# Two FFNs whose up projections keep tokens stationary, in a two-block fp32 kernel on one core

## The chip, the cores and the metric

One core of one Trainium2 chip runs the whole kernel. The metric is device time of one execution in microseconds; the time of a kernel is the median of its runs. The engines are TensorE (PE in the views, its weight loads apart as PEld), VectorE (DVE), ScalarE (ACT), GpSimd (POOL) and SyncE (SP), which issues the DMAs here.

## The reference, cut to what matters

256 tokens of width 1024 go through two blocks. The first has a SwiGLU FFN, a mixer (attention and gated linear attention side by side), a second SwiGLU FFN and a gated embedding; the second block has two more mixers and two FFNs with short convolutions. The change touches the two SwiGLU FFNs and the gated linear attention of the first block:

```python
def swiglu(x, w_gate, w_up, w_down):
    return (jax.nn.silu(x @ w_gate) * (x @ w_up)) @ w_down

h = h + 0.5 * swiglu(rmsnorm(h, ffn1_norm), ffn1_w_gate, ffn1_w_up, ffn1_w_down)   # 1024 -> 2816 -> 1024
...                                                                                  # mixer
h = h + 0.5 * swiglu(rmsnorm(h, ffn2_norm), ffn2_w_gate, ffn2_w_up, ffn2_w_down)

def step(state, inp):            # gated linear attention, one chunk
    qi, ki, vi, gi = inp
    b = jnp.cumsum(gi, axis=2)
    diff = b[:, :, :, None, :] - b[:, :, None, :, :]
    decay = jnp.exp(jnp.where(causal, diff, -jnp.inf))
    attn = jnp.einsum('bhid,bhjd,bhijd->bhij', qi, ki, decay)
    ...
```

## The kernel before, in words

All of it is fp32 in and out. A product of fp32 matrices is made of three matmuls in a reduced format: each operand is split into a high part (`hi` of weights, `xh` of activations) and the rest (`lo`, `xl`), and high x high, high x low and low x high are added in PSUM. Weights arrive in halves of 128 x 1024 values (512 KB): `halves` (L584) issues the DMA into `raw` (3 buffers), ScalarE writes `hi` (L470, AF.Copy), VectorE writes `lo` in two pieces (L436); `hi` and `lo` have six buffers each. The very first half is loaded in four pieces of 128 KB (`PIECES`).

There are two forms of projection. `row_units` (L713) keeps **weights** stationary: a half is 8 k slices of 128 hidden columns, and all 256 tokens of `xh` and `xl` move, so a matmul is 128x256; the result has hidden columns on partitions and tokens along the free axis. `col_units` (L694) keeps **tokens** stationary: a half is two k slices of 512 columns, which move, so a matmul is 128x512, once for each of two token halves; the result has 128 tokens on partitions.

`ffn` (L733) works through 11 groups of 256 hidden columns (`NG`), each with 256 columns of gate and of up weights, and then that group's rows of the down weights:

```python
for g in range(NG + 1):
    if g < na:
        self.run_units(self.col_units(src, up_at[g], 512, xh, xl, tok_fin(g)))
    elif g < NG:
        for c in range(2):
            for run in self.row_units(src, up_at[g] + c, xh, xl, row_fin(2 * g + c)):
                run()
    if g > 0:
        self.run_units(down(g - 1), lead=2 if g == NG else 0)
```

`na` is `NA[0]` for the first FFN and `NA[1]` for the second. After a row unit, `row_fin` (L755) scales the PSUM bank by the tokens' norm factors (VectorE, 128x512; the factors were spread over partitions once by two small matmuls), takes silu of the gate half (ScalarE), multiplies gate and up (POOL, since `TTX` is POOL), and splits the product into `hh` and `hl` (ScalarE and VectorE, tiles `halfr`). After a column unit, `tok_fin` (L738), for each token half, takes silu of the gate columns with the norm factor as ScalarE's scale, multiplies with the up columns on VectorE (tile `half`), transposes the product by two 128x128 matmuls against the identity (L524), and splits the transposed product from PSUM. `down` (L776) uses `hh` and `hl` as stationary operands and moves 512 down-weight columns; it is the same in both cases. The host lays the weights out to suit (`_ffn_w`, L1787), so the bytes loaded are the same.

In the first mixer (`mixer1`, L871) the queries of four heads lie in `gq`, a tile of 128 partitions and two halves of 512, the even heads in partitions 0 to 63 of the first half, the odd ones in partitions 64 to 127 of the second; the rest of the tile is zero. `decay_levels` (L812) multiplies queries and keys by decays at seven levels; for the queries this is one VectorE operation for each of the two halves, on 64 partitions.

The order of all instructions is set by a planner (`Plan`, L53 to L372) when the program is built: it gets every operation with its engine, a cost and its dependencies, lists them in an order for each engine by priority, and chooses the buffer of each tile. Each engine then takes its own instructions strictly in that order. So a change of form anywhere can move instructions elsewhere.

Of the kernel before, what the change touches and what calls it, by code (L numbers as in the profile page):

```python
# [14 lines left out]
P = 128  # L15
# [6 lines left out]
NEG = -1.0e30  # L22
LEVELS = [1, 2, 4, 8, 16, 32, 64]
LEAD = 2
RING = 6
RAW = 3
BANKS = {"a": 8}
BANK = {"m": "a", "t": "a"}
BKEEP = 0
NA = (0, 1)  # L30
RKEEP = 1
HKEEP = 3
OKEEP = 999
# [340 lines left out]
class Kern:  # L374
# [209 lines left out]
    def halves(self, src, idx, width, gain_k=None):  # L584

        def prep(h):
            hw = width // 2
            raw = self.plan.tile("raw", [P, 1024], F32, RAW, RKEEP)
            np_, self.pieces = self.pieces, 1
            for j in range(np_):  # L590
                z = slice(j * hw // np_, (j + 1) * hw // np_)
                self.dma(raw[:, z], src[idx][:, h * hw:(h + 1) * hw][:, z])
            hi = self.plan.tile("hi", [P, 1024], F32R, RING, RKEEP)
            lo = self.plan.tile("lo", [P, 1024], F32R, RING, RKEEP)
            nq = len(LOPAT) // 2
            q = hw // nq
            m = hw // np_
            for j in range(np_):
                self.act(hi[:, j * m:(j + 1) * m], raw[:, j * m:(j + 1) * m], AF.Copy)
            for j in range(nq):  # L600
                s = slice(j * q, (j + 1) * q)
                r = raw[:, j * q:(j + 1) * q]
                self.tt(lo[:, s], r, hi[:, s].bitcast(F32), ALU.subtract, {"P": "POOL", "V": "DVE", "X": "DVE|POOL"}[LOPAT[h * nq + j]])
            return hi, lo

        return [lambda: prep(0), lambda: prep(1)]

    def run_units(self, units, lead=None):
        lead = LEAD if lead is None else lead

        n, w = len(units), {}
        for i in range(n + lead):
            if i < n:
                w[i] = units[i][0]()
                units[i][1](0, *w[i])
            if i >= lead:
                self.plan.bias = BIAS[self.phase]
                units[i - lead][1](1, *w.pop(i - lead))
                self.plan.bias = 0
# [251 lines left out]
    def mixer1(self, xh, xl, rs):  # L871
# [3 lines left out]
        gk, gf = self.big("gk"), self.big("gf")  # L875
        gk3 = gk.rearrange("p (c t) -> p c t", c=2)

        gq = self.plan.tile("g", [P, D], F32, 2)
        self.mset(gq, 0.0)
        gq4 = gq.rearrange("p (n c t) -> p n c t", n=2, c=2)  # L880
        half = [slice(0, 64), slice(64, P)]
# [148 lines left out]
        def og_fin(t, ps):  # L1030
# [9 lines left out]
        self.run_units(self.col_units(a["w_in1"], 0, 512, xh, xl, qk_fin)  # L1040
                       + self.col_units(a["w_in1b"], 0, 272, xh, xl, kv_fin))
        smat = [self.big("smat").rearrange("p (a t i) -> p a t i", a=2, t=2) for _ in range(2)]
        self.decay_levels([(pp, gq[pp, 512 * n:512 * n + 512]) for n, pp in enumerate(half)], gk3, gf,
                          [[(gk3[:, c], gq4[:, :, c], 0)] for c in range(2)], smat)
        self.run_units(self.col_units(a["w_in1"], 2, 512, xh, xl, attn)
                       + self.col_units(a["w_in1"], 4, 512, xh, xl, v_fin)
# [13 lines left out]
        for t in range(2):  # L1060
            po = [self.psum("a") for _ in range(2)]
            os = [po[h % 2][:, 128 * (h // 2):128 * (h // 2) + 128] for h in range(4)]
            for h in (0, 2, 1, 3):
                c, pp = h // 2, slice(64 * (h % 2), 64 * (h % 2) + 64)
# [626 lines left out]
    def run(self):  # L1691
# [21 lines left out]
        def fin1(t, acc):  # L1713
            self.add_half(t, acc)
            self.to_xt(t, self.hsrc(t), *nx, gi=1)
            nr[t] = self.hnorm(t)
        self.ffn(a["w_ffn1"], NA[0], xh, xl, rs, fin1)
        self.phase = 1
# [5 lines left out]
        def fin2(t, acc):  # L1724
            self.add_half(t, acc)
            self.to_xt(t, self.hsrc(t), *px, gi=3)
            pr[t] = self.hnorm(t)
        self.ffn(a["w_ffn2"], NA[1], *nx, nr, fin2)
        self.phase = 3
# [36 lines left out]
def _c(a):  # L1766
    return np.ascontiguousarray(a)
# [7 lines left out]
def _rows2(w):  # L1775

    n = w.shape[0] // 256
    return w.reshape(n, 2, P, D).transpose(0, 2, 1, 3).reshape(n, P, 2 * D)
# [8 lines left out]
def _ffn_w(wg, wu, wd, na):  # L1787
    up, dn = ffn_order()
    out = np.empty((3 * NG, P, 2048), wg.dtype)
    rows = _rows2(wd)  # L1790
    for g in range(NG):
        s = slice(256 * g, 256 * g + 256)
        if g < na:
            out[up[g]:up[g] + 2] = _cols(np.concatenate([wg[:, s], wu[:, s]], 1), 512)
        else:
            z = [slice(256 * g + P * c, 256 * g + P * c + P) for c in range(2)]
            out[up[g]:up[g] + 2] = _stat(np.concatenate([w[:, c] for c in z for w in (wg, wu)], 1))
        out[dn[g]] = rows[g]
    return out
# [10 lines left out]
def layout(i):  # L1810
# [7 lines left out]
        i["ffn1_norm"][0], i["mix_norm"][0], i["ffn2_norm"][0], i["ple_gate_norm"][0])], 1))  # L1818
    o["w_ffn1"] = _ffn_w(i["ffn1_w_gate"][0], i["ffn1_w_up"][0], i["ffn1_w_down"][0], NA[0])
    win = i["w_in"][0]  # L1820
# [13 lines left out]
    o["w_out1"] = _c(_rows2(np.concatenate([wo[:512].reshape(8, 64, D)[order].reshape(512, D), wo[512:]])))  # L1834
    o["w_ffn2"] = _ffn_w(i["ffn2_w_gate"][0], i["ffn2_w_up"][0], i["ffn2_w_down"][0], NA[1])
    wp = i["ple_w_gate"][0]
# [92 lines left out]
```

## Time and profile before

| | |
|---|---|
| median of 3 runs | 1249.11 us (1245.09 to 1250.49) |
| the profiled execution | 1248.71 us |
| its span, first to last instruction | 1246.9 us |
| PE matmul busy | 1218.3 us (98%) |
| DVE, ACT, POOL busy | 857.1 (69%), 672.4 (54%), 194.5 (16%) us |
| read from HBM | 207.18 MB, 167 GB/s over the span |
| ACT table loads | 17 |

By the tiles that PE works on, the first FFN runs from about 7 to 205 us, the first mixer to about 327, the second FFN to about 520. Busy is an engine's time with an instruction in flight. PE's matmuls overlap (one is shown as lasting longer than the distance to the next start), so its pace is read from starts.

### The profile page before, as it was taken

How to read it: one execution, taken by the hardware profiler on the slowest of the kernel's cores; microseconds unless marked ns; L12 is line 12 of the kernel's file. 1: busy time of each engine (PE TensorE's matmuls, PEld its weight loads, DVE VectorE, ACT ScalarE, POOL GpSimd, SP SyncE). 2: the span in 40 equal slices, each digit the busy share in tenths (PEclk: the TensorE clock that was granted, in tenths of full speed). 3: DMA queues.
4: the chain of work that ended last, by engine and by line, in shares of the span. 5: the costliest groups of instructions: out<-in, count | busy, mean ns of one | idle time of the engine just before them, and what ended most of it. 6: DMA issues, size and time to landing. Idle time of an engine off the chain costs nothing.

```text
span 1246.9 us, 21305 instructions
## 1 busy us (share of the span) xinstructions
PE 1218.3 (98%) x8084; PEld 1101.0 (88%) x8084; DVE 857.1 (69%) x1627; ACT 672.4 (54%) x1125; POOL 194.5 (16%) x247
## 2 busy tenths in 40 slices
PE   7999999999999999999999999999999999999997
PEld 7899998787899999789998799999799887999996
DVE  5665567876755655778687786776868557766776
ACT  5444445764654444557465675555652356655554
POOL 2111010420011111002001011111113521111111
PEclk9999999999999999999999999999999999999999
DMA  8755554425455555552424555555553244555552
GB/s 282 231 185 176 189 180 148 143 94 194 161 181 188 187 183 192 180 165 78 146 75 150 195 174 185 181 196 181 187 190 103 80 158 155 185 179 193 187 194 93
DMA packets 61158, 209.61 MB, mean 168 GB/s; under 512 B 7424, under 2 KB 9728, under 8 KB 60928
## 3 DMA queue, kind: packets, MB, share of 16 engines
q1 hardware_dynamic: 61056, 208.26, 50.6%
q8 instruction: 63, 1.03, 0.3%
q14 instruction: 39, 0.32, 0.1%
HBM read 207.18 MB, written 1.05 MB: 167 GB/s over the span
## 4 chain that ended last, share of the span: by engine, by line
PE 79%; DVE 7%; DMA 5%; ACT 4%; issue 2%; POOL 1%; SPq 0%; DVEq 0%; POOLq 0%; ACTq 0%
PE psa L513 77%; DVE lo L436 3%; ACT hi L470 2%; DMA raw<-in_w_ffn 2%; PE psa L524 2%; DVE big L451 1%; DMA raw<-in_cf_u 1%; DVE big L436 1%; POOL sml L436 1%; ACT big L470 1%; DMA raw<-in_w_out 1%; DMA big<-in_xT 1%; ACT L366 1%; DVE xl L436 0%; DVE c_h L451 0%
## 5 line engine op out<-in xcount | busy, mean ns | idle before, releaser
L436 DVE TENSOR_TENSOR lo<-raw,hi 128x512 fp32r<-128x512 f32 x756 | 506.9, 715 | 244.0 <-ACT hi L470 240.7
L470 ACT ACTIVATE hi<-raw 128x1024 fp32r<-128x1024 f32 x381 | 394.0, 1047 | 336.1 <-PE psa L513 237.1
L513 PE MATMUL psa<-xh,hi 128*128 128x256 f32 x1568 | 448.6, 286 | 7.3 <-ACT hi L470 7.0
L513 PE MATMUL psa<-xh,lo 128*128 128x256 f32 x1568 | 445.3, 284 | 1.3 <-DVE lo L436 1.0
L513 PE MATMUL psa<-xl,hi 128*128 128x256 f32 x1568 | 443.7, 283 | 0.1
L513 PEld LDWEIGHTS psa<-xh,hi 128*128 128x128 f32 x1568 | 298.8, 191 | 16.8 <-ACT hi L470 7.4
L513 PEld LDWEIGHTS psa<-xl,hi 128*128 128x128 f32 x1568 | 298.6, 190 | 9.5 <-DVE xl L436 0.4
L513 PEld LDWEIGHTS psa<-xh,lo 128*128 128x128 f32 x1568 | 298.4, 190 | 3.2 <-DVE lo L436 3.1
L513 PE MATMUL psa<-hi,halfr 128*128 128x512 f32 x720 | 212.0, 395 | 0.5 <-DVE halfr L436 0.4
L436 POOL TENSOR_TENSOR big<-big 128x256 f32<-128x256 f32 (+1 forms) x88 | 90.6, 1031 | 597.3 <-ACT big L470 513.0
L513 PE MATMUL psa<-hi,xh 128*128 128x512 f32 (+1 forms) x368 | 144.4, 411 | 2.2 <-ACT xh L470 1.6
L513 PE MATMUL psa<-lo,xh 128*128 128x512 f32 (+1 forms) x368 | 137.5, 392 | 0.9 <-DVE lo L436 0.8
L513 PE MATMUL psa<-hi,xl 128*128 128x512 f32 (+1 forms) x368 | 135.9, 410 | 2.3 <-DVE xl L436 2.2
L513 PEld LDWEIGHTS psa<-hi,halfr 128*128 128x128 f32 x720 | 121.9, 188 | 15.5 <-DVE halfr L436 1.0
L513 PE MATMUL psa<-lo,halfr 128*128 128x512 f32 x360 | 113.6, 391 | 0.5 <-DVE lo L436 0.5
L513 PE MATMUL psa<-big,big 128*128 128x128 f32 (+8 forms) x652 | 92.9, 274 | 1.3 <-DVE big L436 0.9
L513 PEld LDWEIGHTS psa<-big,big 128*128 128x128 f32 (+6 forms) x652 | 86.8, 188 | 8.2 <-POOL big L436 1.5
L513 PEld LDWEIGHTS psa<-hi,xh 128*128 128x128 f32 x368 | 69.2, 190 | 17.0 <-ACT xh L470 4.9
L513 PEld LDWEIGHTS psa<-lo,xh 128*128 128x128 f32 x368 | 69.7, 189 | 15.0 <-DVE lo L436 3.1
L513 PEld LDWEIGHTS psa<-hi,xl 128*128 128x128 f32 x368 | 68.4, 190 | 16.1 <-DVE xl L436 5.1
L513 PEld LDWEIGHTS psa<-lo,halfr 128*128 128x128 f32 x360 | 67.6, 188 | 16.3 <-DVE lo L436 0.9
L470 ACT ACTIVATE big<-big 128x256 f32<-128x256 f32 (+2 forms) x104 | 45.4, 439 | 59.0 <-DVE big L436 35.2
(167 smaller groups left out, 950.2 us busy)
## 6 DMA issues: line engine op xcount, KB each, us to landing
raw<-in_w_ffn SPq DMA_DIRECT2D x131, 512.0 KB, 4.5
raw<-in_cf_u SPq DMA_DIRECT2D x88, 512.0 KB, 4.2
raw<-in_cf_d SPq DMA_DIRECT2D x44, 512.0 KB, 4.3
raw<-in_w_in SPq DMA_DIRECT2D x16, 512.0 KB, 4.6
raw<-in_w_abB SPq DMA_DIRECT2D x16, 512.0 KB, 3.8
raw<-in_w_cA SPq DMA_DIRECT2D x16, 512.0 KB, 3.9
raw<-in_w_cB SPq DMA_DIRECT2D x16, 512.0 KB, 3.8
raw<-in_w_abA SPq DMA_DIRECT2D x12, 512.0 KB, 4.1
```

What stands on the lines that cost most here:

```text
L366: self.nc.scalar.preload_act_table_set(i)
L436: return eng, c, lambda: self.ew(eng).tensor_tensor(out=out, in0=a, in1=b, op=op), op != ALU.pow and not self.ps_(a, b)
L451: lambda: self.nc.vector.scalar_tensor_tensor(out=out, in0=a, scalar=s, in1=b, op0=op0, op1=op1, accum_out=accum),
L470: self.plan.add([("ACT", c, lambda: self.nc.scalar.activation(out, a, f, scale=scale, **kw))], outs, ins, SETS.get(f))
L513: return [self.nc.tensor.matmul(o, l, r, start=st, stop=sp) for o, l, r, st, sp in lst]
L524: self.plan.add([("PE", 4 + P / 1.2, lambda: self.nc.tensor.transpose(out, a, idn))], [out], [a, idn], cols=P * 2)
```

## The change

`NA` goes from (0, 1) to (11, 11): every group of both FFNs goes through `col_units` and `tok_fin`; before, that was so for the first group of the second FFN alone. The norm factors are no longer spread over partitions for the FFNs. The queries' decay takes all 128 partitions of each half of `gq`, zeros among them. The conversion of a weight half into `hi` gets a lower bound on its number of pieces, which is 1.

```diff
+GW = 1
+HIP = 1
-NA = (0, 1)
+NA = (11, 11)
...
             m = hw // np_
-            for j in range(np_):
+            m = min(m, hw // HIP)
+            for j in range(hw // m):
                 self.act(hi[:, j * m:(j + 1) * m], raw[:, j * m:(j + 1) * m], AF.Copy)
...
-        self.decay_levels([(pp, gq[pp, 512 * n:512 * n + 512]) for n, pp in enumerate(half)], gk3, gf,
+        self.decay_levels([(slice(0, P), gq[:, 512 * n:512 * n + 512]) for n in range(2)] if GW else
+                          [(pp, gq[pp, 512 * n:512 * n + 512]) for n, pp in enumerate(half)], gk3, gf,
```

By count, 2016 matmuls of 128x256 leave PE, 1008 of 128x512 and 84 transposes of the product come, and four small matmuls on the norm factors leave. The order changes throughout the first block and in places of the second; the last 1168 PE instructions of the program stand as before. Three places follow. Names are those of tiles with a number of their buffer; L494 before is L496 after, and so on.

SP at the program's start, before (`big_89` to `big_92` take the input, transposed, two k slices each, `big_89` in two loads of one slice; `raw` takes weight halves, `raw_102` the one in four pieces; `c_h` the residual, 1 MB):

```order
L494 DMA big_89<-in_xT 128x256
L494 DMA raw_114<-in_w_ffn 128x1024
L494 DMA raw_102<-in_w_ffn 128x256 x2
L494 DMA big_90<-in_xT 128x512
L494 DMA big_89<-in_xT 128x256
L494 DMA raw_106<-in_w_ffn 128x1024
L494 DMA big_91<-in_xT 128x512
L494 DMA raw_102<-in_w_ffn 128x256 x2
L494 DMA big_92<-in_xT 128x512
L494 DMA c_h_86<-in_x 128x2048
```

The same place after:

```order
L496 DMA big_89<-in_xT 128x256
L496 DMA raw_106<-in_w_ffn 128x1024
L496 DMA raw_102<-in_w_ffn 128x256 x4
L496 DMA raw_109<-in_w_ffn 128x1024
L496 DMA big_89<-in_xT 128x256
L496 DMA big_90<-in_xT 128x512
L496 DMA c_h_86<-in_x 128x2048
L496 DMA raw_102<-in_w_ffn 128x1024
L496 DMA raw_106<-in_w_ffn 128x1024
L496 DMA raw_109<-in_w_ffn 128x1024
L496 DMA big_91<-in_xT 128x512
L496 DMA big_92<-in_xT 128x512
```

The later k slices of the input moved behind the residual and three more weight halves.

PE in the middle of the first FFN, before (`psa` are PSUM banks; `hi` and `lo` here are stationary where `xh` moves, and `halfr` is stationary where they move):

```order
L513 MATMUL psa_117<-hi_103,halfr_129 128x512
L513 MATMUL psa_125<-hi_103,halfr_129 128x512
L513 MATMUL psa_117<-lo_104,halfr_129 128x512
L513 MATMUL psa_125<-lo_104,halfr_129 128x512
L513 MATMUL psa_137<-xh_87,hi_123 128x256
L513 MATMUL psa_137<-xl_88,hi_123 128x256
L513 MATMUL psa_137<-xh_87,lo_119 128x256
```

PE in a middle group after, from the last up matmuls of one token half (on `psa_105`) to its transposes (of `half_131`):

```order
L515 MATMUL psa_105<-lo_128,xh_87 128x512
L515 MATMUL psa_105<-hi_107,xl_88 128x512
L515 MATMUL psa_129<-hi_113,xh_87 128x512
L515 MATMUL psa_129<-lo_111,xh_87 128x512
L515 MATMUL psa_129<-hi_113,xl_88 128x512
L515 MATMUL psa_132<-hi_125,halfr_140 128x512
L515 MATMUL psa_112<-hi_125,halfr_140 128x512
L515 MATMUL psa_132<-lo_108,halfr_140 128x512
L515 MATMUL psa_112<-lo_108,halfr_140 128x512
L526 MATMUL psa_122<-c_ident_62,half_131 128x128 x2
L515 MATMUL psa_129<-hi_113,xh_87 128x512
```

Seven matmuls of 128x512 stand between the last on `psa_105` and the transposes; before, PE had no transposes in such a group.

ACT in middle groups of the first FFN, before (`big<-big` is the silu):

```order
L470 ACTIVATE hi_126<-raw_114 128x1024
L470 ACTIVATE halfr_121<-big_143 128x256
L470 ACTIVATE big_144<-big_144 128x256
L470 ACTIVATE hi_123<-raw_102 128x1024
L470 ACTIVATE big_145<-big_145 128x256
L470 ACTIVATE hi_107<-raw_106 128x1024
```

And after (`half<-psa,sml` is the silu, one for each token half):

```order
L472 ACTIVATE halfr_133<-psa_122 128x256
L472 ACTIVATE half_137<-psa_105,sml_95 128x256
L472 ACTIVATE halfr_140<-psa_122 128x256
L472 ACTIVATE hi_107<-raw_109 128x1024
L472 ACTIVATE hi_110<-raw_102 128x1024
L472 ACTIVATE hi_113<-raw_106 128x1024
L472 ACTIVATE half_115<-psa_129,sml_99 128x256
```

The weight conversions now come in threes between the endings of the two token halves.

## Rows read from the trace of the kernel before

**Rows 1.** The page: busy us of PE by part 1, the chain by part 4.
```profile
PE 1218.3 (98%) x8084; PEld 1101.0 (88%) x8084; DVE 857.1 (69%) x1627; ACT 672.4 (54%) x1125; POOL 194.5 (16%) x247
...
PE 79%; DVE 7%; DMA 5%; ACT 4%; issue 2%; POOL 1%; SPq 0%; DVEq 0%; POOLq 0%; ACTq 0%
```
**Rows 2.** Stretches: length; PE, PEld, DVE, ACT, POOL busy (count); clock; DMA share, GB/s.
```profile
60.00:187.00 127.00, 127.00 (x897) 119.21 (x896) 75.68 (x120) 57.20 (x75) 12.67 (x15) 1.00 0.57 183
...
297.40:311.00 13.60, 13.60 (x59) 11.07 (x60) 8.11 (x16) 5.61 (x8) 0.00 (x0) 1.00 0.58 189
187.00:345.00 158.00, 154.51 (x856) 128.35 (x855) 116.25 (x235) 96.67 (x190) 29.75 (x44) 1.00 0.45 150
500.00:545.00 45.00, 43.19 (x200) 33.82 (x199) 36.64 (x66) 26.91 (x44) 3.68 (x4) 1.00 0.53 170
```
**Rows 3.** Timeline of PE, second FFN: start us, us, engine, line, operation, tiles, shape.
```profile
328.04 0.40 PE L513 MATMUL psa<-hi,xh 128*128 128x512 f32 x1
...
330.33 0.39 PE L513 MATMUL psa<-lo,xh 128*128 128x512 f32 x1
...
335.07 0.28 PE L513 MATMUL psa<-xh,lo 128*128 128x256 f32 x1
...
339.39 0.28 PE L513 MATMUL psa<-xh,lo 128*128 128x256 f32 x1
```
**Rows 4.** Timeline of PE around four transposes at the first mixer's end.
```profile
324.31 0.40 PE L513 MATMUL psa<-lo,xh 128*128 128x512 f32 x1
324.54 0.60 PE L524 MATMUL psa<-c_ident,c_h 128*128 128x128 f32 x4
...
325.21 0.49 PE L524 MATMUL psa<-c_ident,c_h 128*128 128x128 f32 x3
```
**Rows 5.** Second FFN's first group: tile `half` (ns min/median/max), then ACT's and DVE's timeline.
```profile
L470 ACT ACTIVATE half<-psa,sml x2: 458/466/473, 335.2 to 345.8; 128x256 f32<-128x256 f32 x2
L451 DVE SCALAR_TENSOR_TENSOR half<-psa,sml,half x2: 479/481/483, 335.9 to 346.3; 128x256 f32<-128x256 f32 x2
...
351.47 0.38 ACT L470 ACTIVATE halfr<-psa 128x256 fp32r<-128x256 f32 x1 [1.05 <-PE psa L524]
...
351.89 0.42 DVE L436 TENSOR_TENSOR halfr<-psa,halfr 128x256 fp32r<-128x256 f32 x1
```
**Rows 6.** Groups by line, 60 to 187 us: busy us, mean ns | idle before, releaser.
```profile
L470 ACT ACTIVATE big<-big 128x256 f32<-128x256 f32 x15 | 6.1, 409 | 13.1 <-DVE big L436 13.1
...
L436 DVE TENSOR_TENSOR big<-psa,half 128x512 f32<-128x512 f32 x15 | 10.3, 688 | 6.8 <-PE psa L513 6.6
...
L436 POOL TENSOR_TENSOR big<-big 128x256 f32<-128x256 f32 x15 | 12.9, 861 | 115.3 <-ACT big L470 115.3
```
**Rows 7.** Timeline of the start; the last bracket is idle time before and its releaser.
```profile
5.69 1.67 ACT L470 ACTIVATE hi<-raw 128x1024 fp32r<-128x1024 f32 x3 [1.46 <-DMA raw<-in_w_ffn]
...
6.80 0.58 PE L513 MATMUL psa<-xh,hi 128*128 128x256 f32 x1 [6.80 <-ACT hi L470]
...
9.12 0.58 PE L513 MATMUL psa<-xh,hi 128*128 128x256 f32 x1 [0.37 <-DVE xh L445]
...
9.99 1.06 ACT L470 ACTIVATE hi<-raw 128x1024 fp32r<-128x1024 f32 x1 [1.13 <-DMA raw<-in_w_ffn]
...
14.21 0.41 PE L513 MATMUL psa<-xh,hi 128*128 128x256 f32 x1
...
14.42 0.34 PE L513 MATMUL psa<-xl,hi 128*128 128x256 f32 x1
...
14.60 0.28 PE L513 MATMUL psa<-xh,lo 128*128 128x256 f32 x1
...
15.36 0.63 ACT L470 ACTIVATE junkACT<-c_h 128x512 bf16<-128x512 f32 x1 [2.02 <-DMA c_h<-in_x]
...
19.23 0.28 PE L513 MATMUL psa<-xh,lo 128*128 128x256 f32 x1
```
**Rows 8.** The queries' tile `g` on DVE: ns min/median/max, first and last start.
```profile
L436 DVE TENSOR_TENSOR g<-g,half x12: 275/418/775, 253.7 to 271.3; 64x256 f32<-64x256 f32 x10, 64x128 f32<-64x128 f32 x2
```

## The prediction

> **What bounds the kernel now.** I read the page's busy table and its chain first: TensorE's matmul row is busy 98% of the span, and 79% of the chain that ended last is PE, the rest crumbs of other engines [rows 1]. A busy PE row can hide waiting, so the next view is busy time by stretch [rows 2]. In the middle of the first big FFN (60 to 187 us) PE is never idle, while VectorE is busy 75.68 of 127 us (60%) and ScalarE 57.20 (45%). In the stretch from the end of that FFN through the attention/GLA mixer (187 to 345) PE is idle 158.00 - 154.51 = 3.5 us, and where the second FFN hands over to the gate projection (500 to 545) 1.8 us. The granted clock is 1.00 in all four, the higher of TensorE's two levels (2.4 GHz). So the time is PE's instruction stream, and an edit is worth what it adds to or takes from that stream, plus the few microseconds of waits at its edges. What counts there is not a matmul's duration (they overlap) but the distance from one start to the next, which the timeline gives [rows 3].
>
> **The change part by part.**
>
> *Up projections on PE.* 21 of the 22 hidden groups of the two FFNs change form (the second FFN's first group had the new form already). A group was 2 chunks x 2 halves x 8 k x 3 terms = 96 matmuls of 128x256; it becomes 2 token halves x 8 k x 3 = 48 of 128x512. Starts of 128x256: from 335.07 to 339.39 there are 36 of them, 0.120 us each [rows 3]; from 14.60 to 19.23 there are 39, 0.1187 [rows 7]; I take 0.1195. Starts of 128x512 with tokens stationary: 328.04 to 330.33 holds ten, 0.229 [rows 3]; 59 in 13.60 us are 0.2305 [rows 2]; I take 0.231, which leans to the larger sample. Old: 96 x 0.1195 = 11.47 us. New: 48 x 0.231 = 11.09. Gain 0.38 us a group: halving the count while doubling the width is nearly neutral, because a 256-wide one already costs about half.
>
> *Transposes on PE.* The gated product now has tokens on partitions, so each token half needs two 128x128 transposes, 4 a group. Price: from 324.31 to 325.21 stand two 512-wide matmuls and four transposes [rows 4]: 0.90 - 2 x 0.231 = 0.44, or 0.11 each, although each is shown lasting 0.27. Four cost 0.44 us a group. The net is -0.38 + 0.44 = +0.06 a group, +1.3 us for 21. Four small matmuls that spread the token scale over partitions go away in exchange (two per FFN, at the transposes' 0.11): -0.4. **PE work: +0.8 us.** Ends: 0.229 against 0.120 gives -0.09 a group, -2.3 in all; 0.233 (as far above my value as 0.229 is below it) against 0.1187, with 0.12 per transpose, gives +0.27, +5.2 in all.
> The Trainium skill (TensorE: Matmul & The Clock Gate, "Back-to-back issue gap") gives a gap of N/2.4 + 2.5 ns, so 216 ns for 512 columns and 109 for 256; by it, an estimate, the up matmuls would gain only 0.13 a group and the sum would be 5 us higher. The trace has 231 and 120, and its ratio is what I use.
>
> *The other engines.* Per chunk the old ending cost DVE 0.69, ACT 0.41 and POOL 0.86 us [rows 6] ahead of the split into high and low part. The new one costs, per token half, ACT 0.47 and DVE 0.48 [rows 5]; the split stays, one of each per chunk or half (0.38 and 0.42 [rows 5]). Per group of two chunks or two halves DVE falls by 0.4 us, ACT rises by 0.1, POOL loses 1.7. All three lie beside 17 us of PE work per group (11.47 + 24 down matmuls x 0.231) and none is what PE waits for, so I count nothing. Without that cover the 21 groups would give back up to 8 us on DVE.
>
> *The new wait.* A transpose can't start before silu and product are done, and PE takes its instructions in order, so a late product holds up every matmul behind the transpose. After the last up matmul's slot: its data are done 0.16 us later (0.39 long, 0.23 apart), hand-over 0.04 (ScalarE ends at 351.47 + 0.38, VectorE starts at 351.89 [rows 5]), silu 0.47 and hand-over, product 0.48 and hand-over, 0.11 for the transpose's weight load (no more than their spacing): 1.34 us. In the new order on PE (the second of the three places) seven 512-wide matmuls stand between, 1.62 us, for one token half of every steady group of the first FFN; ten in the second; the other half has over 8 us. So the tight case has 0.28 us in hand. From the transpose to the first down matmul that needs it there are six microseconds or more in steady groups. Price 0.
>
> *The start.* The sequence of loads changes (the first of the three places). Before, PE began at 6.80 us, restarted at 9.12 after waiting for the second k slice of x, ran at half pace (starts 0.21 apart at 14.21, against 0.12 later), and only from 14.60 on at full pace [rows 7]: its 29 matmuls by then are 29 x 0.1195 = 3.5 us of work, so it was 11.1 us behind a PE that never waited. After, the first matmul needs the second load's first two pieces: ScalarE converts one full half and two pieces ahead of it, which took from 5.69 to 7.36 before as well: 7.4. The second slice of x is now behind 1,680 KB instead of 1,168. Taking landings by KB ahead as before (1,808 KB in at 9.99, 3,600 at 15.36 [rows 7], so 334 KB per us): it lands at about 10.0, PE resumes at 10.5 instead of 9.12 (conversion and hand-over between), and the slices four and five, behind 4,880 KB, come at about 19.2. PE: 5 matmuls (0.43 each at half pace) to 9.6, wait to 10.5, 12 more at half pace until about 15.8 (the old one needed 5.3 to 5.5 us from its restart to full pace), 7 at full pace to 17.4, 12 of the second group to 20.2, and the slices of x are then there. 36 x 0.231 = 8.3 done at 20.2: 11.9 behind. **+0.8 us**; ends 0 (full pace at 14.6 as before) and +3.4 (the late slices of x 2.6 us later).
>
> *Queries' decay on 128 partitions.* Sixteen VectorE operations (two over 512 elements, twelve over 256, two over 128) work on all partitions, half of them zeros, instead of 64. A 64x256 one takes 0.418 at the median [rows 8], a 128x256 one 0.42 [rows 5]: the price goes by elements per partition, so 0 (at most 0.1 us in all). The slow ones (up to 0.775) are the second of a pair, behind POOL's decay of the keys, and stay. The constant for conversion pieces changes nothing: the minimum is the old value.
>
> *Edges.* The planner sets a new order around both FFN ends. It can at most remove the 3.5 + 1.8 = 5.3 us of PE idle there, or add as much; I take 0.
>
> **Sum against the profiled execution** (1248.71, of which 1246.9 is span): 1248.71 + 0.8 + 0.8 = 1250.3. That execution was 0.4 below the median of the runs, so the forecast is **1250.7**.
>
> **The rivals.**
> 1. *The transposes wait in place* (slower). The silu is one ScalarE instruction in a queue of weight conversions of about 1.06 us. If it becomes ready just after one has begun, the product is up to 1.06 late, 0.28 of which is covered: 0.78 x 21 halves = 16 us, 1267. It decides from 0.28 us of lateness. Against: in the order the silu of the tight half has a short copy ahead of it, three conversions stand before that, and the one group that already has this form shows no PE wait. The old row form had no such point inside a group.
> 2. *A transpose occupies PE for the 0.27 us that its row shows*: 84 x 0.27 = 22.7, less 8.0 for the up matmuls and 0.4, is +14.3, with the start 1264. This is what the Trainium skill (same page, "Part 4: PE-mode transpose") would say, about 275 ns in a kernel's context and no full clock. Against: the starts of rows 4, 0.11 apart with the next matmul not pushed back.
> 3. *Faster*: the new order hands each token half on as soon as it is done, so that the first half's tail, norm and transposes run under the second half's matmuls, and the idle time at both FFN ends goes (-5.3); with the low end of the PE work (-2.3) and the start as before: 1241.5. For it: all of that idle lies at those hand-overs. Against: the order there still has one half's finish just ahead of the mixer's first projections, as before.
>
> **How the numbers follow.** A measurement of this kernel can tell about 0.5% (6.2 us) from no change. Forecast 0.68 (1246 to 1255, all within 0.5%); rival 1 0.14, rival 2 0.04, rival 3 0.14. Faster 0.14, same 0.68, slower 0.18. The range: down to 1243.5, which leaves out the lower part of rival 3 (0.08), and up to 1260, the sum of the upper ends of PE work and start (1248.7 + 5.2 + 3.4 = 1257.3, with under 3 for the edges), which leaves out rival 2 and the full price of rival 1 (0.12).
>
> **What would show it.** Up matmuls of 128x512 starting 0.23 apart and transposes costing 0.11 between them; PE not idle from 60 to 187; no wait of PE on VectorE's product in the waits view; about 20 us until full pace without a gap over 1 us; decay operations of 128x256 at 0.42. Wrong would be: a wait of the same length repeating once every 17 us (rival 1), a group period above 17.3 us without waits (rival 2), or the stretches 187 to 345 and 500 to 545 shortening by several microseconds (rival 3).

## The result, and the profile after

The changed kernel takes 1259.98 us (median of six runs, 1254.16 to 1265.34), the kernel before in the same series 1249.24 (1245.09 to 1250.49): ratio 1.0098, 95% interval 1.0081 to 1.0114. It is slower by about 1%, twice the 0.5% that the prediction took as what a measurement can tell. A later series gave 1258.61 against 1247.77, ratio 1.0086 (1.0073 to 1.0099). The profiled execution is the shortest of its six, 1254.16 (span 1252.3), 5.4 above that of before; a second profile, of the later series, took 1257.38. The loss differs from execution to execution, so I read both profiles.

The page of the changed kernel, parts 1 and 4, answering to [rows 1], and then the stretches of [rows 2]:

```profile
PE 1221.4 (98%) x7152; PEld 1052.4 (84%) x7152; DVE 839.5 (67%) x1627; ACT 670.5 (54%) x1123; POOL 155.1 (12%) x205
...
PE 70%; DMA 11%; DVE 9%; ACT 5%; issue 3%; POOL 1%; SPq 0%; DVEq 0%; POOLq 0%; ACTq 0%
```
```profile
60.00:187.00 127.00, 126.22 (x558) 101.08 (x557) 64.59 (x115) 55.08 (x73) 0.00 (x0) 1.00 0.56 185
187.00:345.00 158.00, 154.71 (x807) 125.64 (x805) 113.09 (x230) 94.49 (x180) 27.90 (x39) 1.00 0.45 147
345.00:500.00 155.00, 153.98 (x683) 122.53 (x682) 83.59 (x153) 73.90 (x106) 3.91 (x7) 1.00 0.56 181
500.00:545.00 45.00, 43.89 (x206) 34.72 (x204) 36.17 (x68) 28.05 (x48) 3.02 (x4) 1.00 0.56 177
```

PE's busy share is the same 98%, the bytes and the clock are the same (in each of the three profiles the granted clock falls to 0.50, the lower level, once and at the same place, near 892, 895 and 897 us, behind an idle PE of 1.7 to 2.0 us), and DVE and POOL have less to do, as forecast. What changed is the chain: PE's share falls from 79% to 70%, and DMA's rises from 5% to 11% (to 16% in the second profile). PE was never idle in the middle of the first FFN; now it is idle 0.78 us there and 1.02 us in the second.

The chain of one 20-us stretch in the middle of the first FFN (start, us, what) shows where it goes. Before, it is one piece, all PE:

```profile
69.93 20.16 PE psa L513 x140
```

In the changed kernel it leads from load to load:

```profile
69.34 6.03 DMA raw<-in_w_ffn
...
75.45 1.06 ACT hi L472
76.51 0.18 ACT halfr L472
76.69 6.44 DMA raw<-in_w_ffn
...
83.22 1.07 ACT hi L472
...
84.31 0.70 DVE lo L438
...
85.05 5.11 PE psa L515 x21
```

A weight half is loaded (6.4 us), split into `hi` (1.07) and `lo` (0.70), and PE has to wait for it; the load itself could only be issued when an earlier conversion had emptied a `raw` buffer. That is what SyncE's queue waits for in this stretch (60 to 187 us; who waits for whom: us, times, longest):

```profile
SPq L496 <- DVE lo L438: 108.9, 44, 7.4
```

Before, it waited as long for the same thing (110.5 us, 45 times); what differs is when the weights are wanted.

Loads of FFN weights, 60 to 187 us (count, KB each, median us from issue to landing), before and after:

```profile
raw<-in_w_ffn SPq DMA_DIRECT2D x45, 512.0 KB, 4.3
```
```profile
raw<-in_w_ffn SPq DMA_DIRECT2D x43, 512.0 KB, 5.3
```

About as many bytes in the same time, but later landings: in the changed kernel the issues come in threes, 1.2 us apart, and then none for 5 us or more (66.94, 68.14, 69.34, then 75.27, 76.69, 77.91 us, then 85.67). The median distance of two issues between 30 and 190 us is 1.24 us; before it was 2.53. The order says why. Counted in PE's work (0.231 and 0.1195 us a matmul), PE wants a new half after 1.4, 1.4, 6.1, 1.8, 1.4 and 4.8 us in a group of the new form, and after 2.1, 5.4, 1.4, 2.8, 2.3 and 2.9 in the old: a half of up weights now lasts six matmuls of one token half, 1.39 us, where it lasted 24 of 128x256, 2.87 us.

By place, from PE's first transposes of the residual after each stage: the first FFN is 1.0 us longer (2.1 in the second profile), the mixer 0.5 shorter (0.6), the second FFN 3.2 longer (3.3), all that follows 1.8 longer (3.9), though no operation changed there.

In the second FFN (327 to 511 us) neither PE nor its weight loads waited for `hi` or `lo` before; now they do:

```profile
PEld psa L515 <- DVE lo L438: 3.9, 9, 0.5
...
PEld psa L515 <- ACT hi L472: 0.8, 3, 0.4
```
```profile
PE psa L515 <- DVE lo L438: 0.8, 4, 0.2
```

In the first FFN, from 30 to 190 us, the waits of PE and of its weight loads for `hi` and `lo` add up to 4.7 us (4.0 in the second profile), but to 3.7 before as well: there the old form is hardly better supplied.

### The profile page after: what moved, and what is told of

Read it like the earlier page. It is cut to its first block, busy times and chain, and to the rows that moved or that the text cites. A ratio compares the mean times of both kernels' runs of the same rounds, so it can differ in the third digit from the quotient of the medians.

```text
span 1252.3 us, 19425 instructions
## 1 busy us (share of the span) xinstructions
PE 1221.4 (98%) x7152; PEld 1052.4 (84%) x7152; DVE 839.5 (67%) x1627; ACT 670.5 (54%) x1123; POOL 155.1 (12%) x205
## 4 chain that ended last, share of the span: by engine, by line
PE 70%; DMA 11%; DVE 9%; ACT 5%; issue 3%; POOL 1%; SPq 0%; DVEq 0%; POOLq 0%; ACTq 0%
PE psa L515 67%; DMA raw<-in_w_ffn 7%; DVE lo L438 4%; ACT hi L472 4%; PE psa L526 3%; DMA raw<-in_cf_u 2%; DVE big L453 1%; POOL sml L438 1%; DMA raw<-in_w_in 1%; DMA raw<-in_w_out 1%; DVE big L438 1%; DMA c_h<-in_x 1%; DVE c_h L453 1%; DVE xl L438 0%; DVE big L486 0%
## 5 line engine op out<-in xcount | busy, mean ns | idle before, releaser
L515 PE MATMUL psa<-hi,xh 128*128 128x512 f32 (+1 forms) x704 | 280.7, 408 | 10.7 <-ACT hi L472 8.0
L515 PE MATMUL psa<-lo,xh 128*128 128x512 f32 (+1 forms) x704 | 272.3, 396 | 1.7 <-DVE lo L438 1.5
L515 PE MATMUL psa<-hi,xl 128*128 128x512 f32 (+1 forms) x704 | 263.2, 406 | 1.7 <-DVE xl L438 1.6
L515 PE MATMUL psa<-xh,hi 128*128 128x256 f32 x896 | 257.1, 287 | 0.1
L515 PE MATMUL psa<-xh,lo 128*128 128x256 f32 x896 | 253.4, 283 | 1.1 <-DVE lo L438 1.1
L515 PE MATMUL psa<-xl,hi 128*128 128x256 f32 x896 | 252.5, 282 | 0.3 <-DVE xl L438 0.3
L515 PEld LDWEIGHTS psa<-xl,hi 128*128 128x128 f32 x896 | 170.1, 190 | 5.4 <-DVE xl L438 0.8
L515 PEld LDWEIGHTS psa<-xh,hi 128*128 128x128 f32 x896 | 169.9, 190 | 4.9 <-ACT hi L472 0.3
L515 PEld LDWEIGHTS psa<-xh,lo 128*128 128x128 f32 x896 | 169.8, 189 | 2.1 <-DVE lo L438 1.9
L515 PEld LDWEIGHTS psa<-hi,xh 128*128 128x128 f32 x704 | 133.1, 190 | 40.4 <-ACT hi L472 10.0
L515 PE MATMUL psa<-lo,halfr 128*128 128x512 f32 x360 | 113.3, 391 | 0.0
```

The source lines that it names most:

```text
L515: return [self.nc.tensor.matmul(o, l, r, start=st, stop=sp) for o, l, r, st, sp in lst]
```

## The experiments

My theory A: the column form wants weights in bursts, so PE waits for halves that land late, differently in each execution. Against it stood B (the order that the planner chose elsewhere, above all in the second block), C (the decay) and D (PE's own work, mis-priced).

**The changed kernel again, and its parts one by one.**

```diff
-NA = (11, 11)
+NA = (0, 1)
```
for the decay alone; for one FFN alone `NA = (11, 1)` or `NA = (0, 11)` with `GW = 0`.

> The changed kernel once more, for its spread and a second profile. Theory A (weight supply): in the column form the first token half takes four new weight halves, 2 MB, in 24 matmuls (24 x 0.231 = 5.5 us), and all four stay in their buffers until the second token half has used them; so PE has little weight in hand and waits whenever a load lands late, a different amount in each execution. Then this profile shows more waits of PE on the weights' hi and lo inside the two FFNs than the first one did (seven of 0.3 to 0.7 us there), the more the longer this execution is; median 1260, spread 8 to 11 us. Theory B (the order around the mixers and in the second block): the additional time lies outside the two FFNs. Theory D (PE's own work mis-priced): the time inside the FFNs is the same in every execution, and so is the total to about 3 us.

> The kernel before with the queries' decay on 128 partitions alone, both FFNs as before. Theories A and D (the FFNs' form): 1249, ratio 1.000 within 0.002. Theory C (the decay, with the order that it makes the planner choose): some or all of the 11 us, 1252 to 1260.

> Only the first FFN in the column form, 11 groups; the second FFN and the decay as before. Theory A: 11 of 21 groups, so about half of the loss, 1254 to 1255, and a wider spread than the kernel before (5 us). Theory D: the same half, but with the spread of the kernel before. Theory B: anything, the loss not in proportion to the groups, and outside 14 to 200 us.

> Only the second FFN in the column form (ten groups more than before); the first FFN and the decay as before. Theory A: about half of the loss, 1254 to 1255, with waits on hi and lo between 345 and 500 us. Theory D: the same half, without such waits. Theory B: the loss not in proportion; with the first-FFN kernel the two do not add up to 11 us.

Measured: 1258.61 again (1257.38 to 1259.73, so the spread was narrow this time, and A's sign is missing: the second profile is 3.2 us longer than the first, but its waits on `hi` and `lo` are not more, 4.0 against 4.7 us in the first FFN and 3.7 against 5.5 in the second); decay alone 1250.86, ratio 1.0027 (1.0012 to 1.0041); first FFN alone 1258.33, 1.0081 (1.0068 to 1.0094); second alone 1253.00, 1.0044 (1.0031 to 1.0056); before 1247.77. The parts, 3.1 + 10.6 + 5.2 us, add up to far more than the whole, 10.8. So A is not all: B has a share. In the profile of the kernel with the first FFN alone, that FFN is 2.1 us longer than before, but the mixer 2.4 and what follows the second FFN 5.7. The decay, which I had priced at nothing, costs 3 us although its operations do not (their median is 0.422 us at 128x256, 0.418 before at 64x256 [rows 8]); in its profile the first block is 1 us shorter than before and what follows 2 us longer.

**Old and new orders put together.** To hold the order of a block fixed, the planner got a list for each engine, made from a plan of the other kernel, and might place an operation of those phases only if it was next on its list.

```diff
+    for x in model.order():
+        if not isinstance(x, str) and x[0] in to:
+            guide[model.ops[x[0]][0][x[1]][0]].append(to[x[0]])
+    trial.guide = guide
     order = trial.order()
...
                 for i in c:
+                    if i in held and self.guide[e][nextg[e]:nextg[e] + 1] != [i]:
+                        continue
```

> The changed kernel, its first block planned as in it, but in the second block (from the second mixer on) every engine takes its instructions in the order of the kernel before. Theory B (a part of the loss is the new order in the second block, where no operation changed): in two profiles of the changed kernel that block is 1.7 and 3.8 us longer than before, so this kernel is 2 to 4 us faster than the changed one, 1254 to 1256. Theory A alone (weight supply in the FFNs): no gain, 1258.

> The other way round: both FFNs, the decay and the first block's order as before, the second block in the order of the changed kernel. Theory B: the second block's share alone, 1250 to 1252. Theory A alone: 1248, the kernel before.

Measured: 1254.75, ratio 1.0059 (1.0043 to 1.0076), and 1248.53, 1.0013 (1.0003 to 1.0023). The old order in the second block gives 3.9 us back, the new order behind the old first block costs 0.8. The first is as B wanted, the second nearer to what A alone wanted: B is there, but it depends on what runs ahead, and 7.1 us remain with the first block's new form and order. One profile each settles no share: in the second kernel's, what follows the second FFN takes 3.2 us more than before, but the first block, with the order of before, ends at 502.5 us in place of 505.3. The stage that stays the same is the old second FFN: 193.8 us in both.

**Half the up bytes, and loads planned as landing later.** These two kept the old second block and let the planner order the first anew.

> As the kernel with the new first and the old second block, but of each half of up weights (all groups but the first) only 256 KB are loaded, and used for both of its k slices: half of the up bytes are left out, all work on the engines stays. Theory A, if the lateness is in the loads' landing: PE's waits on hi and lo inside the FFNs go, and it is 3 to 6 us faster than that kernel, 1249 to 1252. If the weights are late because buffers come back late, or if the loss is PE's own work (theory D): within 1.5 us of that kernel.

```diff
+    Plan.WAIT = {**Plan.WAIT, "SP": (4000,) * 5}
     order = trial.order()
```

> As the kernel with the new first and the old second block, but the planner reckons with 1.6 us more from a load's issue to its landing when it orders the first block (issue to landing is 5.0 us at the median in the changed kernel's FFNs, 4.5 before). Theory A: with an order that expects later weights PE waits less, 1 to 5 us faster than that kernel, 1250 to 1254. Theory D: no change, within 1.5 us.

Measured: 1254.21, as the kernel with full bytes, and 1249.92, ratio 1.0019 (1.0008 to 1.0031). The first looks like a no to A and is not: its first FFN is 5.0 us shorter (195.9 to 200.9), without a wait on weights, but its own order has a wait of PE at the head of the second FFN that the full bytes' order doesn't have (who waits for whom: us, times, longest):

```profile
PE psa L527 <- DVE big L465: 5.7, 1, 5.7
```

So I repeated it below without planning anew. The second says that the lateness can be planned around: no wait of PE in the first FFN, 4.8 us back.

**Is it only a better plan?**

> The control for the run with loads planned late: both FFNs in their old form and the old decay, the first block planned with the same 1.6 us more from a load's issue to its landing, the second block in the order of the kernel before. Theory A (only the column form is short of weights; its loads come in bursts): the old form has nothing to win, 1246 to 1249. If the later landing simply gives a better plan whatever the form: as much faster as the column form became by it (4.8 us), 1243.

> Both FFNs in the column form, planned with the later landing, but the old decay, and the mixers, the gate stage and the second block in the order of the kernel before. Theory A: the weight waits inside the FFNs are gone, and the rest is as before: 1246 to 1249, FFN stages of 196 and 192 to 193 us. If the column form costs something besides weights: above 1250.

Measured: 1250.78, ratio 1.0019 (1.0009 to 1.0029), and 1260.03, 1.0088 (1.0074 to 1.0102). The control came out as A wanted: the old form gains nothing by expecting late loads (it even loses 2.8, more than I had allowed). The second missed by 11 us. In its profile the FFNs take 196.6 and 194.5 us, near what was expected; the mixer is 4.2 us longer than before, and what follows the second FFN 7.8. The granted clock falls to 0.50 at 207.8, 521.8 and 900.7 us, each time behind waits of PE of 1.7 us and more; before, it fell once. Why the old order of the second block does so badly here I do not know. Part of the miss is that the mixer's order, taken from the other form, no longer fits behind the first FFN's tail (the last bracket is idle time before and its releaser):

```profile
205.50 0.66 PE L537 MATMUL psa<-c_ident,c_h 128*128 128x128 f32 x4 [1.74 <-DVE c_h L464]
206.86 0.39 PE L526 MATMUL psa<-hi,xh 128*128 128x272 f32 x1 [0.70 <-ACT hi L483]
```

**Five buffers of `hi` and `lo`.**

```diff
-RING = 6
+RING = 5
```

> The kernel before with five buffers for hi and for lo in place of six. Theory A: the old form takes one half of up weights at a time and gives it back at once, so it loses little, 1249 to 1254.

> The changed kernel with five buffers for hi and for lo in place of six. Theory A: four of the buffers are held by one group's up weights until the second token half has used them, which leaves one in place of two for what comes next, so the loss is several times that of the old form: 20 us or more above the changed kernel, 1280 and up, with PE waiting on hi and lo in every group. If weights are not what PE waits for: as much as the old form loses, 1260 to 1265.

Measured: 1260.08 and 1263.99, ratios 1.0096 (1.0081 to 1.0112) and 1.0126 (1.0110 to 1.0143): the old form loses 12 us, the new one 5 more than it had. I had both sizes wrong. I take from it that the number of converted halves is not what the new form is short of; the planner knows that number and orders around it, and there are fewer issues in a row (2.42 us apart at the median from 30 to 190 us, against 1.24). What it does not know is how late a load lands.

**Half the bytes in exactly the same order.** Only the load is narrower; its planned cost stays, and PE, ACT, DVE and POOL have the same instructions in the same order.

```diff
+                if self.thin:
+                    d, w = raw[:, :hw // 2], src[idx][:, h * hw:h * hw + hw // 2]
+                    self.plan.add([("SP", max(330, self.fsz(raw) * 4 * P / 318.0), lambda: self.nc.sync.dma_start(d, w))], [raw], [w])
+                    continue
```

> The changed kernel with every engine's order exactly as in it; only, of each half of up weights but those of the first group, 256 KB are loaded in place of 512, and what is left in the buffer stands for the rest: half of the up bytes are left out, no instruction and no wait. (The earlier run with half the bytes had an order of its own and a wait of 5.7 us in it.) Theory A1, loads that are issued in threes land late (5.2 us at the median against 4.4 before): landings come down to 3.6, the waits of PE on hi and lo inside the FFNs go, and of the 10.8 us 3 to 6 come back, 1253 to 1256. Theory A2, weights are late because ScalarE and VectorE convert three halves in a row: no change, 1257 to 1260.

> The same in the kernel before, its order exactly as it was, half of the up bytes of both FFNs left out. Its FFNs hardly wait for weights (1.9 us of waits on hi and lo in the first, none in the second). Theory A1: 0 to 2 us faster, 1246 to 1248. If fewer bytes speed up the whole whatever the form: 3 to 6 us faster, 1242 to 1245.

Measured: the new form 1250.85, 7.8 us faster than with all bytes, more than I had expected; the old form 1245.71, 2.1 us faster. Waits from 30 to 190 us (who waits for whom: us, times, longest), in the changed kernel and then with half the bytes:

```profile
ACT hi L472 <- PE psa L515: 45.9, 16, 5.0
...
ACT hi L472 <- DMA raw<-in_w_ffn: 8.0, 12, 2.0
PEld psa L515 <- DVE lo L438: 2.5, 6, 0.5
...
PEld psa L515 <- ACT hi L472: 1.2, 2, 0.9
...
PE psa L515 <- ACT hi L472: 0.5, 1, 0.5
PE psa L515 <- DVE lo L438: 0.5, 2, 0.2
```
```profile
ACT hi L473 <- PE psa L516: 52.6, 19, 5.0
...
ACT hi L473 <- DMA c_ab_cw<-in_ab_cw: 0.8, 1, 0.8
PEld psa L516 <- ACT halfr L473: 0.3, 1, 0.3
```

The conversions still come in threes (they wait for PE to give buffers back, 45.9 and 52.6 us), and yet PE's waits on `hi` and `lo` are gone, with ACT's waits for weight loads. So conversions in a row are not the cause; late landings are. The new form is still 5.1 us behind the old one; by the profiles that is lost in the second block (the table below).

**An even demand.** Without the bias that, in the two FFNs' phases 0 and 2, keeps the second token half behind the first:

```diff
+    old, BIAS = BIAS, [0, BIAS[1], 0] + BIAS[3:]
```

> As the kernel with the new first and the old second block, but in the two FFNs the planner no longer puts the second token half behind the first, so that a new weight half is wanted by PE every 2.5, 2.5, 2.2, 2.4, 0.9 and 6.2 us of its work in a group, in place of 1.4, 1.4, 6.1, 1.8, 1.4 and 4.8 (the kernel before: 2.1, 5.4, 1.4, 2.8, 2.3, 2.9). Nothing is left out. Theory A1: loads are issued further apart, land earlier, the waits on hi and lo inside the FFNs go, 3 to 6 us faster than that kernel (1254.75), 1249 to 1252. Theory A2: the conversions too are spread, the same result. Rival: the token halves now end together and PE waits for silu and product at the transposes, 1256 and up.

Measured: 1266.08, ratio 1.0140 (1.0125 to 1.0155). The time is the rival's; the place is not quite. Weights are no longer late (between 60 and 187 us PE is busy all 127.00, issues are 2.42 us apart), though the first FFN is no shorter for it (200.8 us, 200.9 with the bias). The loss is in the second FFN, 211.7 us in place of 196.4, where PE now waits for the chain behind it, among it the split product at the down matmuls:

```profile
PE psa L526 <- DVE sml L464: 6.5, 1, 6.5
PE psa L526 <- DVE halfr L449: 3.7, 5, 1.5
```

There is no wait for the product at the transposes, where the rival had put it. I read the second line as a use of the bursts: one token half is done early, so that its silu, product, transposes and split run under the other's matmuls. The first line, the longest wait, is put down to a small operation of a norm (`sml`), not to a product.

**A fourth load buffer.** Every order as it was; `raw` gets a fourth buffer, and two kinds of small tiles give up spare ones for it.

```diff
     order = trial.order()
+    trial.recolor({"raw": 4, "sml": 22, "s32": 10})
```

`recolor` gives each tile of these kinds, in the plan's order of time, the buffer that has been free longest.

> The changed kernel, every engine's order exactly as in it, nothing left out; the weight loads go round four buffers (raw) in place of three, the space for which comes from small tiles that had buffers to spare. A load can then be issued one conversion earlier. Theory A1 (late landings are what PE waits for in the FFNs): the waits on hi and lo there go, as with half the bytes (1250.85): 1250 to 1254. If a fourth load in flight only makes all of them land later still, or if it is not the landing: 1257 to 1260.

> The kernel before, its order exactly as it was, with the same fourth load buffer. Theory A1: it has few waits on weights to lose, as with half the bytes (2.1 us): 1245 to 1248.

> Both FFNs in the column form, the first block planned with the later landing, the second block in the old order (that was 1249.9), and the fourth load buffer. The account so far: PE's own work in the FFNs falls by 2 to 3 us, the weight waits are gone, the second block is as before: 1244 to 1248, at best a little faster than the kernel before. If something of the column form is still unaccounted for: 1249 or more.

Measured: the new form **1240.16** (1239.67 to 1241.27), ratio to the kernel before 0.9941 (0.9928 to 0.9954); the old form 1241.55 (1239.82 to 1243.06), 0.9951 (0.9937 to 0.9965); the third 1246.40, 0.9987 (0.9977 to 0.9997). One buffer takes 18.4 us from the changed kernel, far more than I expected, and 5.9 from the one before, more too (all projections load through `raw`, those of the second block as well). The new form with it is 0.6% faster than the kernel before, and it is no longer slower than the old form with the same buffer (their ranges overlap). Its chain, on the page and in the stretch from 70 to 90 us:

```profile
PE 88%; DVE 6%; issue 2%; POOL 2%; ACT 1%; DMA 0%; SPq 0%; DVEq 0%; POOLq 0%; ACTq 0%
```
```profile
71.60 7.46 PE psa L530 x32
79.06 0.22 PE psa L541 x2
79.28 9.20 PE psa L530 x40
```

and its loads between 60 and 187 us:

```profile
raw<-in_w_ffn SPq DMA_DIRECT2D x42, 512.0 KB, 5.1
```

They still land late, 5.1 us after issue, and still come in threes (1.21 us apart); but each waits for a conversion one earlier, and so is issued earlier. Of 40 conversions between 60 and 187 us 13 began within 0.12 us of their load's landing in the changed kernel, 8 in the kernel before, none with half the bytes or with four buffers; the median load lies landed 0.9 us before its conversion in the changed kernel and 3.1 with four buffers. DMA leaves the chain.

By place, in us. Each row is one profile, and places of one order differ by over a microsecond between profiles; only the old second FFN is the same, 193.8, in all four profiles with the order of before (these three and that of the exchanged orders).

| | first FFN | mixer | second FFN | the rest |
|---|---|---|---|---|
| before | 197.8 | 113.8 | 193.8 | 741.5 |
| changed, two profiles | 198.7, 199.9 | 113.3, 113.2 | 197.0, 197.0 | 743.4, 745.4 |
| half the bytes, old form | 194.7 | 113.2 | 193.8 | 741.9 |
| half the bytes, new form | 195.6 | 112.4 | 193.0 | 745.1 |
| four load buffers, old form | 194.3 | 111.6 | 193.8 | 738.3 |
| four load buffers, new form | 194.5 | 110.6 | 192.6 | 741.7 |

In the second FFN the new form alone loses 3.2 us, and both amends give them back and more. In the first, both forms gain: 3.0 and 3.4 us the old one, 3.1 to 5.4 the new one. The rest takes 3.2 and 3.4 us more in the new order in the pairs with half the bytes and with four buffers; I read that share as the order's. The third kernel, with the order that expects late loads, is slower than the first, which was planned without. I read this as the cost of that order itself, which is left once loads have lead; it was not tried apart.

## Why the prediction was wrong

The forecast was 1250.7, no change that can be told; the time lies just inside the range (to 1260), and that is luck: its upper end was made of dearer PE work and a later start, neither came, and none of the three rivals is how the time came there. Step by step:

- **The other engines: wrong, and the step that failed.** "All three lie beside 17 us of PE work per group and none is what PE waits for, so I count nothing." The sums per group were right (DVE and POOL fell), but a sum per group does not say when within it a half is wanted. And the loads have no term at all outside the start, though the same bytes are wanted in another rhythm. Rows of before would have given a warning: a half of up weights lasts 1.39 us in the new form (six matmuls of 0.231), and in the profile before a load took 4.3 us, a conversion 1.06 [rows 7], and there were three buffers for loads. Half the bytes in the same order is worth 7.8 us here and 2.1 before; one more load buffer 18.4 and 5.9, which takes the whole loss away. Where it is plainest is the second FFN: 193.8 us before, 197.0 after, 192.6 with four buffers.
- **PE work: right, and a little too dear.** I had +0.8 us. 128x256 start 0.1195 us apart, 128x512 0.231 in the first FFN and 0.228 in the second. The pair of transposes costs what I took for it, 0.22 us, but over a third of that shows only behind it:

```profile
79.98 0.62 PE L515 MATMUL psa<-lo,halfr 128*128 128x512 f32 x2
80.44 0.38 PE L526 MATMUL psa<-c_ident,half 128*128 128x128 f32 x2
80.58 0.48 PE L515 MATMUL psa<-hi,xh 128*128 128x512 f32 x1
80.89 0.39 PE L515 MATMUL psa<-lo,xh 128*128 128x512 f32 x1
```

  Up to the start of the next matmul the pair adds 0.60 - 2 x 0.231 = 0.14; but that matmul then takes 0.31 to the next start in place of 0.231: 0.91 - 3 x 0.231 = 0.22 in all, as the chain above has it (0.22, x2). Without waits (four load buffers) a group takes 17.08 us in the first FFN and 16.86 in the second, against 17.0 in the old form (96 x 0.1195 + 24 x 0.231). And the four small matmuls on the norm factors are eight records of PE, so that they were worth about 0.9 us and not 0.4. So PE's work falls by 1 to 2 us; with four load buffers first FFN, mixer and second FFN take 497.7 us in the new form and 499.7 in the old, in the two profiles.
- **The new wait: right in the steady groups, not in the first.** No wait of PE on the product in 60 to 187 us. But in the first group PE waits for it, 0.2 us in one profile and 1.7 in the other. The chain of that other one:

```profile
18.97 5.80 DMA raw<-in_w_ffn
...
24.87 1.07 ACT hi L472
...
25.96 0.69 DVE lo L438
26.66 0.41 DVE half L453
...
27.11 0.44 PE psa L526 x2
```

  It is rival 1's mechanism (the silu stands behind a weight conversion in ScalarE's queue, the product behind the `lo` of the same half in VectorE's), but what sets it off is the load for which that conversion waits. With half the bytes or four buffers it is gone.
- **The start: right in kind, too dear.** First matmul at 7.53 (forecast 7.4), but no wait for the second slice of x, where I had 0.9 us, and full pace from 14.2 in place of 15.8. Counted as lag behind the work done, PE is 11.0 us behind at 20 us, as before (11.2 in the second profile): 0 to 0.2 of the +0.8.
- **The decay and the edges: the price right, the place not.** The decay's operations cost nothing more, but the kernel with it alone is 3.1 us slower, 2 of it, in one profile, behind the second FFN. "Edges 0" was too narrow a view of what a new order can do: I bounded it by the idle time at the FFN ends alone, and some 3 us are lost in the second block, where no operation changed.
- **Rivals.** 2 did not show: 0.27 us is what a row says of a transpose's length, and its place in PE's order costs 0.11. (The Trainium skill, TensorE: Matmul & The Clock Gate, "Part 4: PE-mode transpose", has about 275 ns; the trace agrees for the length alone.) 3 did not show either: from 500 to 545 us PE's idle time fell from 1.8 to 1.1, from 187 to 345 from 3.5 to 3.3. 1 came only as said, in the first group.

Where the distance of two starts of PE exceeds the median of the first one's form by more than 0.3 us, I count the excess as lost. That is 22.3 us before, 24.9 and 29.1 in the two profiles after, 22.1 with half the bytes, 16.7 with four buffers (16.2 in the old form). So such waits are 12.4 of the 16.1 us between the second profile and that with four buffers (1241.27). Of them 5.4 are waits on `hi` and `lo` (6.5 to 1.1); the others are waits on other results of ScalarE and VectorE, whose queues also hold the conversions. That a late conversion holds those up is shown for the 1.7 us above; for the rest it is argued.

**Open.** How the 10.8 us divide is settled only roughly: about 3 in the second FFN for late loads, 2 to 4 in the second block for its order (0.8 and 3.9 by the two kernels with exchanged orders), the remainder in the first FFN, where profiles of one order differ by over a microsecond. The parts built alone do not add. The new form with four load buffers, planned as usual, and the second block in its old order was not run. That the landing time makes the spread from run to run (1254 to 1265 in one series, 1257 to 1260 in another) is argued, not shown, and the second profile's waits on weights speak against it. More buffers for `hi` and `lo` were not tried, for want of room.

## What to carry to other kernels

When an edit changes how long an operand stays in use, write down at what intervals the next one is wanted, and set that against issue to landing plus conversion and the number of load buffers; a mean rate and a busy share show nothing of it. A load's lead is set by the buffer that it waits for, so before a form is judged, try it with one more load buffer, for the old form too. And where a planner orders everything, test a part with the order held fixed: a part planned anew brings waits of its own.

## What was not expected of the hardware

- The 128x512 matmuls of the second FFN start 0.2285 us apart, those of the first 0.2313 (means without waits in the profile after; 0.2278 and 0.2312 with four load buffers), with the granted clock at 1.00 in both. The down matmuls do not differ (0.229 in both); the up matmuls do (0.233 and 0.228). I have no reason for it.
- Two 128x128 transposes between 128x512 matmuls are shown as 0.27 us long each. The second starts 0.11 us after the first, and the next matmul 0.03 after the second, but that matmul keeps PE for 0.316 us in place of 0.231 (means of 15 pairs of the first FFN in the profile after). Whoever stops counting at its start gets 0.14 for the pair and not 0.22.
- A wait of PE costs more than its length. In the kernel with even demand PE, which had been busy without a break at a clock of 1.00, stood still for 6.5 us, until 359.8; the granted clock then fell to 0.50, the lower level, and came back at about 365, and in between matmuls of 128x512 started 0.43 us apart (stretch, us, then busy by engine, clock, DMA):

```profile
345.00:352.80 7.80, 7.80 (x36) 6.47 (x35) 4.07 (x7) 3.38 (x4) 0.00 (x0) 1.00 0.67 223
352.80:359.50 6.70, 0.46 (x3) 0.04 (x1) 3.49 (x7) 4.73 (x11) 0.56 (x1) 0.69 0.63 200
359.50:365.00 5.50, 5.19 (x12) 4.12 (x13) 3.17 (x9) 4.55 (x10) 2.40 (x5) 0.50 0.25 88
365.00:370.00 5.00, 5.00 (x24) 4.09 (x23) 2.47 (x6) 1.97 (x4) 0.56 (x2) 0.94 0.09 19
```
- Three loads of 512 KB issued 1.2 us apart land 3.8, 6.0 and 6.0 us after issue (66.94 to 70.74, 68.14 to 74.14, 69.34 to 75.37), while the mean rate is the same as before.
